# GpSimd takes eight weight splits and the pooling sums, the convolution sums in PSUM, and a layer norm's sums move into the stage before

## The chip, the cores and the metric

The kernel runs on one NeuronCore of a Trainium2 chip, with fp32 inputs and outputs. The metric is the device time of one execution in microseconds (us); lower is better. The kernel before was timed in 3 runs; one further execution was recorded by the hardware profiler.

## What is computed

The program is a stack of two layers (a retention layer, then a latent-attention layer, each followed by a per-layer embedding gate `x = x + sigmoid(x @ w_gate) * proj`) and then a second block with adaptive modulation. The change lies at the end of the second gate and in the first half of the second block, on 256 tokens of 1024 features. With `mod` worked out from a conditioning vector, that half computes:

```python
h  = layer_norm(x) * (1 + scale_1) + shift_1
z  = h @ w_in2                       # 4 x 512 channels: a, b for the GLU, c for the pool, then 2048 gates
u  = a * sigmoid(b)                  # GLU, 512 channels
v  = causal_depthwise_conv(u, 31 taps) + b_dw
v  = silu(layer_norm(v, g_a, b_a)) @ w_pw
q_g = sums of 2, 4, 8, 16 past tokens / width - c    # one group of 128 channels per width
q  = (q @ w_pool) * pool_scale
m  = sigmoid(gates_1) * v + sigmoid(gates_2) * q
x  = layer_norm(alpha * x + g_1 * (m @ w_out2), g, b)   # alpha = 2 ** 0.25
```

## The kernel before

Activations lie with features on the 128 partitions and the 256 tokens along the free axis, in blocks of 4 x 256 columns (tiles `half`). Weights come from DRAM in 258 tiles of 128 x 1024 fp32 (tiles `raw`), in one order, by DMAs that SyncE issues (L165). A tile holds eight 128 x 128 weights.

A product is made in one of two ways. An **fp32 tile** goes to TensorE as it is, one fp32 matmul for each weight (`mm32`, L243). A **split tile** is first taken apart: ScalarE casts it to fp32r (`hi`, tile `wh`, L178), VectorE subtracts that from the original (`lo`, tile `wl`, L179), and each product then is three fp32r matmuls, `hi` by `hi`, `hi` by `lo` and `lo` by `hi` (`mm`, L237 to L239). The raw tiles have 6 buffers, `wh` and `wl` 5 each; every second fp32 tile (by its place in the DRAM order) lies in a buffer of `wh`.

The stages around the change, in the order of TensorE's work:

- `ple_gate1`: eight output blocks; for each, `fin` (L697 to L699) takes a sigmoid on ScalarE, then a product and a sum on VectorE that give the new `x`. Blocks come in pairs (0,1), (2,3), (4,5) and then 6 and 7 alone.
- the part of `w_in2` that needs no norm yet (`ahead_mm`, L1011): 4 blocks of `w_in2` times `x * scale` (written by ScalarE at L1036), 32 fp32 matmuls of 258 columns. The layer norm's sums over `x` and its squares (`ln_sums`, L973; `sum_mm`, L363; matmuls with a matrix of ones) come in between, due 4.16 us of the program's own clock after the stage's beginning. Then `ln_stats`, `modulate` (L981) and `glu_ahead` (L1109), which takes the mean and the factor into the blocks that were multiplied ahead.
- `k_outer` (L1025): four split tiles, the other two channel groups of the GLU.
- the pool's two pairs of blocks, called P0 and P1 here (two tiles each), and the eight gates G0 to G7 (two tiles each, `in_tile` L1129), with `pool_out` (four small products with `w_pool`) after G3. Of these only G2, G5 and G6 are split (the bits of the number 100). Each gate ends with a sigmoid of 512 columns out of its PSUM bank (L1210).
- beside them the convolution (`conv_steps`, L1075): 2 channel pairs x 31 taps, one step each 0.9 us of the program's clock. A step is two multiplications on ScalarE (L1087) and one addition of 512 columns on VectorE (L1088), or, for some steps, two fused multiply-adds on VectorE (L1091). Its sums lie in SBUF.
- the pool (`pool`, L1145): 1, 2, 3 and 4 shifted additions on VectorE (L1150), then a tail of three operations (L1152, L1154, L1155) and a split (L187, L188) for `pool_out`.
- the norm of the convolution's result (`ln_a`; its first half's sums at L1170 in G2, the second's at L1178 in G7), then `w_pw` and `w_out2`. For the residual, `alpha * x` is written by ScalarE ahead of the convolution (`ax`, L1120).

GpSimd has hardly any work here: it clears 16 columns ahead of each pool tile (L1065).

The order within an engine comes from a queue of due times (`after(us, fn)`, read by `tick`, which TensorE's work moves forward) and from a scheduler that then places the recorded instructions. PSUM has 8 banks (`bank`, `bank2`).

## Time and profile before

| | |
|---|---|
| runs | 840.65, 841.06, 841.72 us; median 841.06 us |
| profiled execution | 839.76 us, of which the trace spans 838.0 us |
| granted TensorE clock | 0.996 of full speed |
| TensorE busy | 822.8 us, 98% of the span |
| VectorE, ScalarE, GpSimd busy | 84%, 66%, 1% |
| matmuls | L237, L238, L239: 1504 each of 256 columns; L243: 384 |

The profiled execution is read for durations and for who waits for whom; a row gives the start, the time, the engine, the line, the operation and the tiles. Rows of the same kind that follow each other are put together (x4). In the windows the busy share of each engine stands beside the stretch's length.

### The profile page before, as it was taken

To read this page: it belongs to the slowest core of one execution; us is meant where nothing else is said; L and a number is where in the kernel's file an instruction comes from. 1 tells how busy PE (TensorE), PEld (TensorE's weight loads), DVE (VectorE), ACT (ScalarE), POOL (GpSimd) and SP (SyncE) were. 2 spreads that over 40 slices of the span, in tenths; PEclk is the share of its full clock that TensorE was granted. 3 is DMA by queue.
4 is the path that set the end of the run, shared out by engine and by line. 5 is a ranking of instruction groups with operands and counts; after the bars stand their busy time and mean duration, and the time that the engine had idled before them with its cause. 6 is when DMAs were issued, how large, how long until landed. Compare 5 with 4: busy or idle time off the path is not lost.

```text
span 838.0 us, 15757 instructions
## 1 busy us (share of the span) xinstructions
PE 822.8 (98%) x6114; PEld 786.4 (94%) x6114; DVE 701.5 (84%) x1283; ACT 550.6 (66%) x966; POOL 9.9 (1%) x30
## 2 busy tenths in 40 slices
...
GB/s 332 328 249 228 205 228 271 248 261 316 174 174 241 273 135 286 111 224 198 114 175 187 116 201 180 72 176 199 129 250 121 136 195 180 190 211 240 285 80 76
DMA packets 46635, 167.49 MB, mean 200 GB/s; under 512 B 5216, under 2 KB 5472, under 8 KB 46560
## 3 DMA queue, kind: packets, MB, share of 16 engines
...
HBM read 165.41 MB, written 1.05 MB: 199 GB/s over the span
## 4 chain that ended last, share of the span: by engine, by line
PE 85%; DVE 7%; DMA 5%; ACT 1%; issue 1%; SPq 0%; DVEq 0%; POOL 0%; POOLq 0%; ACTq 0%
PE ps L238 24%; PE ps L239 23%; PE ps L237 23%; PE ps L243 11%; DVE wl L179 2%; DMA adach<-in_wada 1%; PE ps L341 1%; DMA g<-mod 1%; PE ps L363 1%; DMA half<-in_rows 1%; DMA half<-in_xT 1%; PE ps L920 1%; ACT wh L178 1%; DMA raw<-in_wts 1%; DMA half<-g 1%
## 5 line engine op out<-in xcount | busy, mean ns | idle before, releaser
L237 PE MATMUL ps<-half,wh 128*128 128x256 f32 x1504 | 424.9, 283 | 0.1
L238 PE MATMUL ps<-half,wh 128*128 128x256 f32 x1504 | 423.3, 282 | 0.7 <-DVE half L188 0.6
L239 PE MATMUL ps<-half,wl 128*128 128x256 f32 x1504 | 421.8, 281 | 0.0
L178 ACT CAST wh<-raw 128x1024 fp32r<-128x1024 f32 x233 | 243.2, 1049 | 147.4 <-PE ps L238 99.0
L179 DVE TENSOR_TENSOR wl<-raw,wh 128x1024 fp32r<-128x1024 f32 x233 | 282.2, 1218 | 55.4 <-ACT wh L178 53.6
L238 PEld LDWEIGHTS ps<-half,wh 128*128 128x128 f32 x1504 | 283.2, 188 | 2.0 <-DVE half L188 1.0
L237 PEld LDWEIGHTS ps<-half,wh 128*128 128x128 f32 x1504 | 282.7, 188 | 1.2 <-ACT half L187 0.5
L239 PEld LDWEIGHTS ps<-half,wl 128*128 128x128 f32 x1504 | 283.6, 189 | 0.0
L243 PE MATMUL ps<-half,raw 128*128 128x256 f32 (+2 forms) x384 | 84.9, 380 | 0.0
L243 PEld LDWEIGHTS ps<-half,raw 128*128 128x128 f32 x384 | 72.5, 190 | 10.0
L237 PE MATMUL ps<-wh,half 128*128 128x512 f32 (+1 forms) x202 | 72.6, 360 | 1.2 <-ACT wh L178 1.2
L238 PE MATMUL ps<-wl,half 128*128 128x512 f32 (+1 forms) x202 | 70.9, 351 | 0.5 <-DVE wl L179 0.5
L239 PE MATMUL ps<-wh,half 128*128 128x512 f32 (+1 forms) x202 | 71.0, 351 | 0.0
L413 DVE CUSTOM_DVE_ANT_0 adach<-adach,siluc 128x1024 f32<-128x1024 f32 x48 | 58.4, 1219 | 14.0 <-DMA adach<-in_wada 13.8
L1087 ACT ACTIVATE t<-apad,vec 128x256 f32<-128x256 f32 x106 | 44.2, 498 | 0.5 <-DVE half L1088 0.5
L237 PEld LDWEIGHTS ps<-wh,half 128*128 128x128 f32 x202 | 37.9, 188 | 7.0 <-ACT wh L178 2.0
L238 PEld LDWEIGHTS ps<-wl,half 128*128 128x128 f32 x202 | 38.1, 189 | 6.0 <-DVE wl L179 1.0
L239 PEld LDWEIGHTS ps<-wh,half 128*128 128x128 f32 x202 | 38.0, 188 | 5.5
L1088 DVE TENSOR_TENSOR half<-half,t 128x512 f32<-128x512 f32 x53 | 36.4, 686 | 3.7 <-ACT t L1087 1.8
L187 ACT CAST half<-t 128x256 fp32r<-128x256 f32 (+1 forms) x47 | 20.3, 453 | 14.3 <-DVE t L1347 11.1
L188 DVE TENSOR_TENSOR half<-t,half 128x256 fp32r<-128x256 f32 (+1 forms) x47 | 21.6, 481 | 4.3 <-ACT half L187 3.4
L1342 ACT ACTIVATE t<-ps,vec 128x256 f32<-128x256 f32 x38 | 21.0, 558 | 4.2 <-DVE t L1344 2.9
...
## 6 DMA issues: line engine op xcount, KB each, us to landing
raw<-in_wts SPq DMA_DIRECT2D x257, 512.0 KB, 4.3
adach<-in_wada SPq DMA_DIRECT2D x48, 512.0 KB, 5.3
...
half<-in_rows POOLq DMA_DIRECT2D x2, 512.0 KB, 5.6
...
siluc<-in_cv SPq DMA_DIRECT2D x1, 512.0 KB, 8.4
```

Of the source, the lines that this page charges most:

```text
L178: A.copy(hi, raw)
L179: V.tensor_sub(lo, raw, hi.bitcast(F32))
L187: A.copy(hi, src)
L188: V.tensor_sub(lo, src, hi.bitcast(F32))
L237: T.matmul(ps, l[0], r[0], start=first, stop=False)
L238: T.matmul(ps, l[0], r[1], start=False, stop=False)
L239: T.matmul(ps, l[1], r[0], start=False, stop=last)
L243: T.matmul(ps, w, r, start=first, stop=last)
L413: V.tensor_tensor_reduce(ch, ch, sc, 1.0, 0.0, MUL, ADD, mod[:, n:n + 1])
L1087: A.activation(t[:, b, :], apad[:, i0 + b, k:k + S], AF.Copy, scale=w[b])
L1088: V.tensor_add(acc.pair(i0 // 2), acc.pair(i0 // 2), t)
L1342: A.activation(t[:, b, :], ps[:, b, :], AF.Identity, bias=col("b_dw_f_2", m), scale=w[2])
```

## The change

- **Splits on GpSimd.** `load` takes a pair of engines (`by`). With `(G, G)` GpSimd casts the tile and subtracts. That holds for eight tiles: P1's two and those of G1, G3 and G5. Before, P1, G1 and G3 were fp32 tiles (six) and G5 was split by ScalarE and VectorE. G2 and G6 stay as they were; P0, G0, G4 and G7 stay fp32.
- **Pooling sums on GpSimd.** The 10 shifted additions of 256 columns.
- **Convolution in PSUM.** Each channel pair's sums lie in a PSUM bank of their own (`accp`); only the last tap writes to SBUF.
- **The norm's sums fed early.** `fin` of `ple_gate1` hands each new piece of `x` to a running sum (`Sums.feed`: a square on ScalarE, additions on VectorE). `flush` is due 4.16 us after blocks 4 and 5: it runs an `Abs_reciprocal_sqrt` on one column (`warm`), folds the two sums of squares into one in place, and starts the matmuls with ones. Blocks 6 and 7 come in by `end`. Six matmuls take the place of eight.
- **Alpha out of the residual.** `ax` goes; `w_out2`'s result is scaled by `g_1 / alpha`, and the next norm's epsilon by `1 / alpha ** 2`.
- **Gates ahead.** `modulate` of blocks 0 to 5 comes first, then `glu_ahead` for both blocks, then the rest.

```diff
     def load(entries, width, parts=True, raw=None, by=None):
...
-        A.copy(hi, raw)
-        V.tensor_sub(lo, raw, hi.bitcast(F32))
+        first, second = by or (A, V)
+        if first is G:
+            G.tensor_copy(hi, raw)
+        else:
+            A.copy(hi, raw)
+        second.tensor_sub(lo, raw, hi.bitcast(F32))
...
+    sumt = Sums(True, 1)
+    st = {}
+
+    def seen(x, k):
+        if k < 6:
+            sumt.feed(x)
+            if k == 4:
+                after(4.16, sumt.flush)
+        elif k == 6:
+            after(2.2, lambda: sumt.end(x, False))
+        else:
+            after(2.3, lambda: stats_in(x))
...
-    after(4.16, stats_in)
     pab = ahead_mm("w_in2", [0, 4, 1, 5], xs, 2)
...
-    modulate(xt, 0, mu, nrl, range(2), hp, hraw)
+    modulate(xt, 0, mu, nrl, range(3), hp, hraw)
...
     acc = Blk(4)
+    accp = [bank2() for _ in range(2)]
...
+            own = accp[i0 // 2]
...
+                to = acc.pair(i0 // 2) if k == 30 else own
...
-                    V.tensor_add(acc.pair(i0 // 2), acc.pair(i0 // 2), t)
+                    V.tensor_add(to, own, t)
...
     glu_ahead(0)
-    modulate(xt, 0, mu, nrl, range(2, 4), hp, hraw)
     glu_ahead(1)
-    ax = Blk(DB)
-    for i in range(4):
-        A.activation(ax.pair(i), xt.pair(i), AF.Copy, scale=ALPHA)
+    modulate(xt, 0, mu, nrl, range(3, 4), hp, hraw)
...
-            in_tile(ps[:, b, :], 8 + 2 * i + b, False)
+            in_tile(ps[:, b, :], 8 + 2 * i + b, i > 0, (G, G))
...
-            V.tensor_add(n[:, 16:], s[:, 16:], s[:, 16 - (1 << i):16 + S - (1 << i)])
+            G.tensor_add(n[:, 16:], s[:, 16:], s[:, 16 - (1 << i):16 + S - (1 << i)])
...
-        in_tile(ps[:, b, :], 12 + 2 * j + b, bool(100 >> i & 1))
+        in_tile(ps[:, b, :], 12 + 2 * j + b, i not in (0, 4, 7), (G, G) if i % 2 else None)
...
+    V.tensor_scalar(ga, mod[:, 16:24], 1.0 / ALPHA, None, MUL)
...
-            V.scalar_tensor_tensor(z[k], ps[:, b, :], mod[:, 16 + k:17 + k], ax[k], MUL, ADD)
+            V.scalar_tensor_tensor(z[k], ps[:, b, :], ga[:, k:k + 1], xt[k], MUL, ADD)
...
-        st["z"] = ln_stats(sumz.ps[::-1], D)
+        st["z"] = ln_stats(sumz.ps[::-1], D, (eps_a, LN_EPS / ALPHA ** 2))
```

What this does to the order of the instructions is shown at three places. Line numbers in these rows are those of the kernel they come from; the numbers behind names tell buffers apart.

**TensorE and ScalarE where `ple_gate1` ends.** On TensorE before: in the middle of `ahead_mm` (`ps_6373` to `ps_6376`, L243) stand the eight matmuls with ones; `ps_6391` takes the sums of `x`, `ps_6392` those of its squares.

```order
L243 MATMUL ps_6373<-half_6359,raw_6387 128x258 [waits Activation_49]
L243 MATMUL ps_6374<-half_6359,raw_6387 128x258
L363 MATMUL ps_6391<-t_1134_6403,ones 128x256 [waits DVE_49,PE_49]
L363 MATMUL ps_6391<-t_1134_6403,ones 128x256
L363 MATMUL ps_6391<-half_6086,ones 128x256 x2
L363 MATMUL ps_6392<-t_1130_6393,ones 128x256 [waits PE_49]
L363 MATMUL ps_6392<-t_1130_6393,ones 128x256
L363 MATMUL ps_6392<-t_1133_6401,ones 128x256 [waits Activation_49]
L363 MATMUL ps_6392<-t_1133_6401,ones 128x256
L243 MATMUL ps_6375<-half_6359,raw_6387 128x258
```

In the changed kernel, right behind the last matmul of `ple_gate1` (L244 into `ps_6330`); `ps_6355` takes the squares' sums (`t_1101` is the folded tile), `ps_6356` those of `x`; L248 is `ahead_mm`.

```order
L244 MATMUL ps_6330<-half_6060,wl_6334 128x256
L339 MATMUL ps_6355<-t_1101_6215,ones 128x256 [waits DVE_49,PE_49]
L339 MATMUL ps_6356<-t_1104_6224,ones 128x256 [waits PE_49]
L339 MATMUL ps_6355<-t_1126_6366,ones 128x256 [waits Activation_49]
L339 MATMUL ps_6356<-half_6088,ones 128x256
L248 MATMUL ps_6398<-half_6384,raw_6402 128x258 [waits DMAHW7_49,PE_49]
L248 MATMUL ps_6399<-half_6384,raw_6402 128x258 [waits PE_49]
L248 MATMUL ps_6400<-half_6384,raw_6402 128x258 [waits PE_49]
L248 MATMUL ps_6401<-half_6384,raw_6402 128x258 [waits PE_49]
L248 MATMUL ps_6398<-half_6384,raw_6402 128x258
L248 MATMUL ps_6399<-half_6384,raw_6402 128x258
L339 MATMUL ps_6355<-t_1135_6410,ones 128x256 [waits Activation_49]
```

Four of the matmuls with ones now stand ahead of all of `ahead_mm` and the first of them waits for VectorE; the last two follow six matmuls later. On ScalarE before, around the sigmoid of block 7 (L697), with the multiplications by `scale` (L1036) and the squares (L296):

```order
L1036 ACTIVATE half_6359<-half_6085,s_6352 128x256
L697 ACTIVATE t_1119_6348<-ps_6317 128x256 [waits PE_49]
L1036 ACTIVATE half_6360<-half_6086,s_6352 128x256 [waits DVE_49]
L1036 ACTIVATE half_6360<-half_6086,s_6352 128x256
L1036 ACTIVATE half_6360<-half_6086,s_6352 128x256 [waits DVE_49] x2
L296 ACTIVATE t_1130_6393<-half_6085 128x512
L296 ACTIVATE t_1131_6395<-half_6085 128x512
L296 ACTIVATE t_1132_6398<-half_6086 128x512
```

and in the changed kernel (L1046 the multiplications, L315 `warm`, which reads the tile `t_1101` that the fold writes, L355 the squares of blocks 6 and 7, L695 the sigmoid):

```order
L1046 ACTIVATE half_6384<-half_6087,s_6377 128x256 x3
L315 ACT_TABLE_LOAD
L315 ACTIVATE sm_6357<-t_1101_6215,eps_r 128x1 [waits DVE_49]
L355 ACTIVATE t_1126_6366<-half_6088 128x256 [waits DVE_49,Activation_49]
L695 ACT_TABLE_LOAD
L695 ACTIVATE t_1127_6373<-ps_6330 128x256 [waits PE_49]
L1046 ACTIVATE half_6384<-half_6087,s_6377 128x256
L1046 ACTIVATE half_6385<-half_6088,s_6377 128x256 x3
L1046 ACTIVATE half_6385<-half_6088,s_6377 128x256 [waits DVE_49]
L355 ACTIVATE t_1135_6410<-half_6088 128x256 [waits Activation_49]
```

Two loads of an activation table stand around `warm`, one ahead of it and one ahead of block 7's sigmoid; before there was none between the sigmoids.

**GpSimd, and VectorE ahead of G2.** On GpSimd in the changed kernel, from G1's second tile (`wh_6936`, `wl_6937`) on; `lv` are the pool's tiles, `upad` its input:

```order
L181 CAST wh_6936<-raw_6934 128x1024 [waits DMAHW1_49,DMAHW7_49,DMAHW0_49,PE_49]
L184 TENSOR_TENSOR wl_6937<-raw_6934,wh_6936 128x1024 [waits Pool_49]
L1155 TENSOR_TENSOR lv_6868<-upad 128x256 [waits Activation_49]
L1155 TENSOR_TENSOR lv_6946<-upad 128x256 [waits Activation_49]
L1069 MEMSET lv_6949 128x16 [waits DVE_49,Pool_49]
L1155 TENSOR_TENSOR lv_6949<-lv_6946 128x256 [waits Pool_49]
L1069 MEMSET lv_7064 128x16 [waits Pool_49]
L1069 MEMSET lv_7067 128x16 [waits DVE_49]
L1155 TENSOR_TENSOR lv_7064<-upad 128x256 [waits Activation_49]
L1155 TENSOR_TENSOR lv_7067<-lv_7064 128x256 [waits Pool_49]
L1069 MEMSET lv_7070 128x16 [waits Pool_49]
L1155 TENSOR_TENSOR lv_7070<-lv_7067 128x256
```

Before, GpSimd had in this stretch only the MEMSETs of 16 columns:

```order
L1065 MEMSET lv_6875 128x16 [waits DVE_49]
L1065 MEMSET lv_6955 128x16 [waits DVE_49]
L1065 MEMSET lv_6958 128x16 [waits DVE_49,Pool_49]
L1065 MEMSET lv_6961 128x16 [waits DVE_49]
L1065 MEMSET lv_7035 128x16 [waits DVE_49]
```

Behind these rows the changed kernel has the rest of the pool's additions, then the casts and subtractions for G3 and G5. On VectorE before, ahead of the subtraction for G2's first tile (`wl_6909`):

```order
L1155 TENSOR_TENSOR half_6791<-sm_6965,upad 128x16 [waits DVE_49]
L1150 TENSOR_TENSOR lv_7038<-lv_7035 128x256 [waits DVE_49,Pool_49]
L1088 TENSOR_TENSOR half_6482<-half_6482,t_1231_6867 128x512 [waits DVE_49]
L1091 SCALAR_TENSOR_TENSOR half_6482<-apad,vec,half_6482 128x256 [waits Activation_49]
L1088 TENSOR_TENSOR half_6482<-half_6482,t_1236_6888 128x512 [waits DVE_49]
L179 TENSOR_TENSOR wl_6909<-raw_6906,wh_6908 128x1024 [waits DMAHW6_49,Activation_49]
L1088 TENSOR_TENSOR half_6482<-half_6482,t_1237_6895 128x512 [waits DVE_49]
```

and in the changed kernel, ahead of the same subtraction (now `wl_6991`; `lv_7196` is the last of the pool's tiles that GpSimd writes, L1097 a convolution step):

```order
L1157 SCALAR_TENSOR_TENSOR half_6833<-lv_7196,upad 128x240 [waits Pool_49]
L1097 TENSOR_TENSOR ps_6498<-ps_6498,t_1232_6884 128x512 [waits DVE_49,Activation_49]
L193 TENSOR_TENSOR half_6837<-half_6833,half_6836 128x256 [waits Activation_49]
L1097 TENSOR_TENSOR ps_6498<-ps_6498,t_1237_6901 128x512 [waits DVE_49]
L1159 TENSOR_TENSOR sm_7200<-lv_7196,cst 128x16
L1237 TENSOR_SCALAR sm_7674<-gs 128x8
L1097 TENSOR_TENSOR ps_6498<-ps_6498,t_1238_6914 128x512 [waits DVE_49]
L1160 TENSOR_TENSOR half_6833<-sm_7200,upad 128x16 [waits DVE_49]
L1238 SCALAR_TENSOR_TENSOR sm_7674<-s_6377,vec 128x8
L1097 TENSOR_TENSOR ps_6498<-ps_6498,t_1239_6927 128x512 [waits DVE_49]
L184 TENSOR_TENSOR wl_6991<-raw_6988,wh_6990 128x1024 [waits DMAHW1_49,PE_49,Activation_49]
```

Before, the pool's additions (L1150) were VectorE's own and its fourth tail came behind this subtraction; now all four tails stand ahead of it, the fourth waits for GpSimd, and the convolution's steps write `ps_6498`.

**TensorE where G4 begins.** Before, the last product of `pool_out` (`ps_7107`) and G4 (`ps_7120`):

```order
L239 MATMUL ps_7107<-half_6794,wl_7070 128x256
L237 MATMUL ps_7107<-half_6794,wh_7069 128x256
L238 MATMUL ps_7107<-half_6795,wh_7069 128x256
L239 MATMUL ps_7107<-half_6794,wl_7070 128x256
L243 MATMUL ps_7120<-half_6454,raw_7121 128x256 [waits DMAHW6_49,Activation_49]
```

and in the changed kernel (`ps_7229`, `ps_7242`):

```order
L244 MATMUL ps_7229<-half_6836,wl_7174 128x256
L242 MATMUL ps_7229<-half_6836,wh_7173 128x256
L243 MATMUL ps_7229<-half_6837,wh_7173 128x256
L244 MATMUL ps_7229<-half_6836,wl_7174 128x256
L248 MATMUL ps_7242<-half_6460,raw_7243 128x256 [waits DMAHW7_49,Activation_49]
```

In both, G4's first matmul waits for ScalarE, whose sigmoid frees the PSUM bank. By the built programs' bank numbers `ps_7120` had G2's bank (`ps_6905`), while `ps_7242` has G3's (`ps_7090`), the one that was filled just before `pool_out`.

## Rows read from the trace of the kernel before

**Rows 1.** Parts 1, 4 and 6 of the page: busy time, share of the span and instructions of TensorE; the chain of work that ended last, by engine; and from part 6 SyncE's DMAs of weight tiles (count, KB each, median us from issue to landing).

```profile
PE 822.8 (98%) x6114; PEld 786.4 (94%) x6114; DVE 701.5 (84%) x1283; ACT 550.6 (66%) x966; POOL 9.9 (1%) x30
...
PE 85%; DVE 7%; DMA 5%; ACT 1%; issue 1%; SPq 0%; DVEq 0%; POOL 0%; POOLq 0%; ACTq 0%
...
raw<-in_wts SPq DMA_DIRECT2D x257, 512.0 KB, 4.3
```

**Rows 2.** The windows of the stretches: the norm's stage, `k_outer`, P0 and P1, G0 and G1 (length, busy time and instructions of each engine, granted clock, DMA share, GB/s).

```profile
496.62:514.13 17.51, 17.51 (x82) 15.11 (x82) 13.71 (x25) 12.88 (x30) 0.00 (x0) 1.00 0.45 151
514.13:525.43 11.30, 11.30 (x97) 11.30 (x97) 6.60 (x17) 11.27 (x28) 0.00 (x0) 1.00 0.54 187
525.43:539.25 13.82, 13.82 (x66) 12.17 (x65) 12.65 (x25) 13.67 (x36) 0.12 (x1) 1.00 0.12 39
539.25:552.68 13.43, 13.43 (x64) 11.80 (x63) 13.43 (x33) 13.01 (x31) 0.67 (x6) 1.00 0.33 118
```

**Rows 3.** The chain of waits, in order of time (start, us, what): the longest pieces between 496 and 554 us. Every fp32 matmul is recorded as two, so x128 are the 64 matmuls of eight tiles, and x16 are eight sums.

```profile
496.62 6.10 PE ps L243 x28
502.71 3.58 PE ps L363 x16
506.29 7.83 PE ps L243 x36
525.43 27.63 PE ps L243 x128
```

**Rows 4.** ScalarE's timeline at the end of `ple_gate1` and in the norm's stage (start, us; in brackets idle time before it and what ended it).

```profile
493.72 1.05 ACT L178 CAST wh<-raw 128x1024 fp32r<-128x1024 f32 x1 [1.32 <-issue]
...
494.68 0.37 ACT L697 ACTIVATE t<-ps 128x256 f32<-128x256 f32 x1
494.95 0.28 ACT L1008 COPY half<-s 128x4 f32<-128x4 f32 x2
...
495.32 1.70 ACT L1036 ACTIVATE half<-half,s 128x256 f32<-128x256 f32 x4
...
505.28 1.28 ACT L393 ACT_TABLE_LOAD   x1
...
509.93 0.60 ACT L991 ACTIVATE half<-t,mod,ms 128x256 fp32r<-128x256 f32 x1 [2.14 <-DVE t L987]
```

**Rows 5.** VectorE's timeline in the same place: the last sums that give `x`.

```profile
493.81 0.69 DVE L699 TENSOR_TENSOR half<-t,half 128x512 f32<-128x512 f32 x1
...
497.32 0.42 DVE L698 TENSOR_TENSOR t<-t,half 128x256 f32<-128x256 f32 x1 [0.50 <-ACT t L697]
497.79 0.42 DVE L699 TENSOR_TENSOR half<-t,half 128x256 f32<-128x256 f32 x1
```

**Rows 6.** ScalarE's groups by line and shape (busy us, mean ns of one, idle before): casts of weights and `warm` over the whole span, `ax` and the norm's squares from 484 to 600 us.

```profile
L178 ACT CAST wh<-raw 128x1024 fp32r<-128x1024 f32 x233 | 243.2, 1049 | 147.4 <-PE ps L238 99.0 <-issue 24.2 <-PE ps L239 15.0
...
L317 ACT ACTIVATE sm<-t,eps_r 128x1 f32<-128x1 f32 x4 | 1.2, 306 | 0.0
...
L1120 ACT ACTIVATE half<-half 128x512 f32<-128x512 f32 x4 | 2.3, 625 | 0.0
...
L296 ACT ACTIVATE t<-half 128x512 f32<-128x512 f32 x4 | 2.2, 616 | 0.0
```

**Rows 7.** VectorE's groups over the whole span: the convolution's additions, the fused multiply-adds, the weights' subtractions, a pool addition, and an addition that reads PSUM.

```profile
L1088 DVE TENSOR_TENSOR half<-half,t 128x512 f32<-128x512 f32 x53 | 36.4, 686 | 3.7 <-ACT t L1087 1.8
...
L179 DVE TENSOR_TENSOR wl<-raw,wh 128x1024 fp32r<-128x1024 f32 x233 | 282.2, 1218 | 55.4 <-ACT wh L178 53.6
...
L1091 DVE SCALAR_TENSOR_TENSOR half<-apad,vec,half 128x256 f32<-128x256 f32 x14 | 6.2, 478 | 0.2
...
L1150 DVE TENSOR_TENSOR lv<-lv 128x256 f32<-128x256 f32 x6 | 2.5, 414 | 0.0
...
L548 DVE SCALAR_TENSOR_TENSOR t<-ps,t 128x512 f32<-128x512 f32 x8 | 5.5, 684 | 0.3 <-PE ps L239 0.3
```

**Rows 8.** GpSimd's operations: the only two that read and compute (minimum, median and maximum ns of one), and two forms of MEMSET.

```profile
L1432 POOL TENSOR_TENSOR t<-t,half x2: 1253/1495/1737, 828.6 to 830.3; 128x512 f32<-128x512 f32 x2
...
L767 POOL MEMSET kr<- 64x256 f32 x4 | 1.2, 306 | 149.0 <-DVE t L560 148.8
...
L1065 POOL MEMSET lv<- 128x16 f32 x10 | 1.1, 112 | 134.1 <-DVE sm L1154 122.1 <-DVE lv L1150 12.0
```

**Rows 9.** The timelines of GpSimd and VectorE around those two operations.

```profile
828.58 2.96 POOL L1432 TENSOR_TENSOR t<-t,half 128x512 f32<-128x512 f32 x2 [11.89 <-DVE t L1431]
...
827.81 1.38 DVE L1431 TENSOR_TENSOR t<-t,half 128x512 f32<-128x512 f32 x2
...
831.31 0.77 DVE L1434 SCALAR_TENSOR_TENSOR t<-t,sm,half 128x512 f32<-128x512 f32 x1
...
832.08 0.74 DVE L1434 SCALAR_TENSOR_TENSOR t<-t,sm,half 128x512 f32<-128x512 f32 x1
```

**Rows 10.** Around the gates: VectorE's subtraction for G2's first tile, on ScalarE the square of the convolution's first half and the sigmoid of G3, and on TensorE the beginning of `w_pw`.

```profile
550.76 1.21 DVE L179 TENSOR_TENSOR wl<-raw,wh 128x1024 fp32r<-128x1024 f32 x1
...
552.66 0.63 ACT L1165 ACTIVATE t<-half 128x512 f32<-128x512 f32 x1 [0.32 <-DVE half L1088]
...
568.44 0.58 ACT L1210 ACTIVATE half<-ps 128x512 f32<-128x512 f32 x1
...
597.13 0.73 PE L237 MATMUL ps<-half,wh 128*128 128x256 f32 x4
```

53 lines of the change are left out of this document (22 added, 31 removed).

## The prediction

> **What bounds the kernel now.** I read the page's busy shares and its chain first: TensorE is busy 98% of the span, and 85% of the chain of waits is TensorE's [rows 1]. So the time is TensorE's work plus its waits, and an edit counts only by what it does to these. Then the windows of the changed stretch: TensorE works without a gap from 496.62 to 552.68, at a granted clock of 1.00, the 2.4 GHz level [rows 2]. In the same windows ScalarE has 13.67 of 13.82 us and VectorE 13.43 of 13.43: they are nearly full, so a delay on one of them soon reaches TensorE. Last the chain by pieces, for the price of a matmul in each form [rows 3].
>
> **Six tiles split (P1, G1, G3).** Eight fp32 tiles take 27.63 us in a row [rows 3], 3.454 each. `k_outer` does four split tiles in 11.30 us [rows 2], 2.825 each. The difference is 0.629, six times that is **-3.77 us**, all of it on TensorE's path if no wait takes its place. G5 is split already; moving its two splits takes 2 casts of 1.05 [rows 6] from ScalarE and 2 subtractions of 1.22 [rows 7] from VectorE, nothing from TensorE.
>
> **The norm's stage.** The eight sums take 3.58 us [rows 3], 0.448 each; six take 2.68, so -0.90. The 32 products of `ahead_mm` (6.10 + 7.83 us [rows 3], 0.435 each) stay. But four sums now stand ahead of all of them, and the first waits for the fold, which writes in place what `warm` reads, and `warm` needs its table. Laying out ScalarE's rows in the new order: the cast from 493.72 ends at 494.8 [rows 4]; the square of blocks 4 and 5 takes 0.62 [rows 6], its input is there at 494.50 [rows 5], so 495.4; the sigmoid of block 6 takes 0.37 and the four copies 0.37 [rows 4], which brings it to 496.1; three multiplications at 0.41 (four in 1.70 [rows 4]) to 497.2 or 497.3; the table 1.28 [rows 4] to 498.5; `warm` 0.31 [rows 6] to 498.8; the fold 0.42 like the addition of that size [rows 5] to 499.2. TensorE is there at 496.62 and **waits 2.6 us**. Then four sums (501.0), six products (503.6), two sums (504.5) and 26 products: `k_outer` starts at 515.8, where it was 514.13. The term is **+1.7 us**. It can't be much more, since after that the stage runs on TensorE alone (the first `modulate`, at 509.93 before [rows 4], gets its sums some 1.8 us sooner). Its lower end is a fold that waits for VectorE alone, with block 6's sum shortly before block 7's product at 497.32 [rows 5]: a wait of about 1.1, a term of +0.2; with no wait at all, -0.9. I take 1.7, since the order shows the wait.
>
> [...]
>
> **Convolution in PSUM, alpha, gates ahead.** A VectorE operation of 512 columns takes 684 ns with an input in PSUM and 686 without [rows 7]; one that also writes PSUM isn't in the trace. I take no difference. Were each of the 53 additions 10% slower, the convolution would end 3.6 us later, by which the second half of `ln_a` would hold `w_pw` up; that end is in the range. `ax` (four copies of 0.62 [rows 6]) goes from ScalarE, where it stood ahead of the first tap, so the convolution can begin two us sooner against the start of `k_outer`. That cancels the later start; I cost both at nothing. The new scale factor is one small operation.
>
> **GpSimd's own time.** Two inputs of 512 columns took it 1253 ns without company [rows 8], 2.45 ns a column; a MEMSET 306 ns for 256 columns and 112 for 16 [rows 8], 0.81 ns a column. So an estimate of 2.4 us for a subtraction of 1024 columns and 0.65 to 0.7 for a pool addition. A cast has one input: between 0.93 (MEMSET's slope) and 2.4 (two inputs). I take 1.1, as one input is nearer to the MEMSET, with 2.4 as the other end.
>
> Does this hide? P1's tiles: the buffers come free as `k_outer` goes through its tiles (from 518.6 every 2.8 us), a split takes 3.5, and TensorE is at P1 at 515.8 + 11.3 + 6.9 = 534.0. G1's: the second needs the `wh` buffer of P0's first tile (free at 530.6) and is done at 534.1, needed at 549.4. Then the pool: three additions on P0's output, seven on P1's (there at 539.7, plus copies), with their MEMSETs, end near 546, and the fourth tail on VectorE follows. G2's subtraction stands behind that tail: 550.1 to 551.3, against 550.76 before [rows 10]. TensorE needs it at 515.8 + 11.3 + 13.8 + 11.3 = 552.2. **It hides, with 0.9 us to spare.** If the cover goes, TensorE waits at G2 for the excess. SyncE's order is the same, but its issues for G2's and G3's tiles now wait for GpSimd's subtractions of P1 and G1 (526 and 534) where they waited for TensorE; a tile lands 4.3 us after its issue [rows 1], before the casts for G2 and G3 come up (some 546).
>
> **G4's PSUM bank.** G4 now takes the bank of G3, whose sigmoid must first be done. Before, from the square of the convolution's first half (552.66) to that sigmoid (568.44) ScalarE took 15.78 us [rows 10]; now two more multiplications and one cast and one half split fewer lie between, some 15.4. The first half ends at about 553.1 (its last taps stand behind the fourth tail), so the sigmoid ends near 569.1 (0.58 [rows 10]). TensorE reaches G4 at 552.2 + four tiles 11.3 + sums 1.7 + `pool_out` 2.8 = 568.0: **+1.1 us**, between 0 and 1.7.
>
> **The sum.** 839.76 - 3.77 + 1.7 + 1.1 = 838.8 for an execution like the profiled one. The runs' median lies 1.30 above it (841.06), so **840.1 us**: 0.1% faster than before. A difference under 0.2% (839.4 to 842.7) can't be told from none.
>
> **Rivals.**
>
> *Short waits, a plain gain.* If the fold waits for VectorE only (+0.2) and ScalarE reaches G3's sigmoid in time (0), the sum is 839.76 - 3.57 + 1.30 = 837.5. With no wait in the norm's stage it would be 836.4. For it: all windows show an ordered flow, and the additions and subtractions that leave VectorE (10 x 0.41 and 2 x 1.22 [rows 7]) are 6.5 us of slack. Against it: the tables stand in the order.
>
> *GpSimd and VectorE block each other (slower).* The first two-input operation of GpSimd began at 828.58, while VectorE's second of two with both inputs in SBUF ran to 829.19; the two took 2.96 together, one 1253 and one 1737 [rows 8, 9]. The excess of 0.48 is close to the 0.6 that VectorE still had to go. Against it: VectorE's 831.31 began 0.23 before GpSimd's end and took 0.77 against the next one's 0.74 [rows 9]. The convolution's steps have one input in PSUM and would be spared; the pool's tails, the splits for `pool_out` and G2's subtractions, some 13 operations with two SBUF inputs between 534 and 553, are the ones that meet GpSimd's additions and G3's casts. Half an addition (0.35) at ten of them and half a cast or a subtraction (0.6 to 1.2) at the others give about 5 us on VectorE's queue, of which 0.9 is spare: TensorE waits 4 us at G2, the sum is 844.2. It decides from a delay of 0.9 us on.
>
> "SBUF — State Buffer" of the Trainium skill, section "Who interferes with whom", states this rule: a VectorE instruction with two SBUF inputs and a GpSimd instruction that reads SBUF exclude each other for a whole instruction, whichever came first, and one with at most one SBUF input is free. The trace agrees on GpSimd's side (1737 against 1253 ns) and doesn't on VectorE's (0.77 against 0.74).
>
> *GpSimd is slow.* With 2.4 for a cast and 2.7 for a subtraction the four splits of P1 and G1 run back to back from 518.6 at 5.1 each to 538.9, the pool's additions start 4.2 later, G2's subtraction ends 3.7 after TensorE wants it, and the sum is 843.8.
>
> *It doesn't do what it says.* That the fed sums bring nothing, since TensorE then waits for them, is part of the forecast already.
>
> **How the numbers follow.** The forecast (840.1; its own range 838.2 to 842, which takes in 0.2 to 2.2 for the norm's stage and 0 to 1.7 for the bank) has 0.42, a third of it under 839.4, as its lower bounds reach further than its upper ones. Short waits 0.25. Blocking 0.20, a quarter of it under 842.7. Slow GpSimd 0.10. Slow writes to PSUM (843.7 by the 3.6 us above) 0.03. So faster is 0.14 + 0.25 = 0.39, slower 0.15 + 0.10 + 0.03 = 0.28, and no difference that can be told 0.33. The range reaches from 836.4, the sum without a wait in the norm's stage or at G4, to 845.0, a little over the blocking.
>
> **What would show it.** The norm's stage: a TensorE wait for the fold of about 2.6 us right after `ple_gate1`, and three table loads on ScalarE between 494 and 508. The tiles: P1, G1 and G3 at 5.65 us each. The hiding: no TensorE wait at P1, G1, G2 or G3, and GpSimd's cast near 1.1 us. The bank: a wait of about 1 us of G4 for ScalarE. Blocking would show as VectorE's pool tails and subtractions longer than 0.4 and 1.22, or late without a visible releaser, and a wait at G2 for `wl`. The prediction falls if the stretch from 496.6 to `w_pw` (597.1 before [rows 10]) changes by over 3 us either way.

## The result, and the profile after

| | before | changed |
|---|---|---|
| runs | 841.39 us median (840.65 to 842.26, 4 runs) | 851.65 us median (850.58 to 853.36, 4 runs) |
| profiled span | 838.0 us | 851.6 us |
| `ple_gate1`'s last matmul to `w_pw` | 496.62 to 597.13: 100.51 us | 497.95 to 610.12: 112.17 us |

The ratio is 1.0133, with a 95% interval from 1.0116 to 1.0151: 1.3% slower. Where `ple_gate1` ends varies by some us (495.48 to 501.91 in profiled executions of kernels that are alike up to there), so the stretch from there to `w_pw` is the better measure, and below each run is read by it (called the stretch). It grew by 11.66 us, in place of shrinking by about 1. One execution of each kernel gives it, so it isn't exact either: p1_fp32 below has a stretch 4.7 us shorter than the changed kernel's, and a median only 1.0 us lower.

The page's part 1 of the changed kernel, which answers to [rows 1]:

```profile
PE 825.5 (97%) x6158; PEld 790.3 (93%) x6158; DVE 709.1 (83%) x1275; ACT 549.8 (65%) x964; POOL 44.2 (5%) x56
```

TensorE has fewer fp32 matmuls and yet 2.7 us more busy time, and GpSimd's 44.2 us are no large share. What TensorE waited for, between 480 and 620 us (the engine's instructions, released by; us in total, times, longest):

```profile
PE ps L244 <- DVE wl L184: 6.0, 1, 6.0
PE ps L339 <- DVE t L348: 2.7, 1, 2.7
PE ps L242 <- ACT half L192: 1.4, 1, 1.4
PE ps L243 <- DVE half L1008: 1.2, 1, 1.2
```

Four waits, where there was none before: at G2 for VectorE's `lo` (6.0), at the sums for the fold (2.7), at `w_pw` (1.4) and in `k_outer` (1.2). And the windows (columns as in [rows 2]; the granted clock stands third from the end), cut at these waits:

```profile
497.95:500.69 2.74, 0.00 (x1) 0.03 (x1) 1.78 (x5) 2.69 (x6) 0.00 (x0) 1.00 0.50 190
500.69:504.25 3.56, 3.56 (x9) 2.85 (x10) 0.85 (x2) 3.55 (x8) 0.00 (x0) 0.53 0.00 1
504.25:519.00 14.75, 14.75 (x69) 12.87 (x69) 10.48 (x18) 9.32 (x17) 0.00 (x0) 1.00 0.40 143
...
557.10:563.36 6.26, 0.23 (x3) 0.03 (x2) 6.26 (x9) 2.33 (x5) 4.36 (x2) 0.92 0.00 0
563.36:566.00 2.64, 2.64 (x12) 2.64 (x13) 2.64 (x5) 1.08 (x3) 0.00 (x0) 0.50 0.55 200
566.00:572.10 6.10, 6.10 (x36) 5.92 (x34) 5.75 (x11) 6.10 (x15) 0.00 (x0) 0.74 0.88 340
```

After the waits of 2.7 and 6.0 us TensorE works at 0.53 and 0.50 of full speed for some us, the 1.2 GHz level, and 0.74 is a window with both levels. What that costs is busy time times the missing share: 3.56 x 0.47 + 2.64 x 0.50 + 6.10 x 0.26 = 4.6 us. With the waits (2.74 + 1.2 + 6.03 + 1.39 = 11.4) that is 16.0; the splits (-3.77) and the two sums saved (-0.90) leave 11.3 of the 11.66 us.

Why VectorE was late at G2 is read from its timeline beside GpSimd's, in `k_outer`. VectorE:

```profile
521.43 0.75 DVE L1061 SCALAR_TENSOR_TENSOR t<-t,t 128x256 f32<-128x256 f32 x2
522.10 0.86 DVE L1060 SCALAR_TENSOR_TENSOR t<-t,sm,ps 128x256 f32<-128x256 f32 x2
522.88 3.01 DVE L1061 SCALAR_TENSOR_TENSOR t<-t,t 128x256 f32<-128x256 f32 x2
525.81 1.26 DVE L1008 TENSOR_TENSOR half<-half,half 128x256 fp32r<-128x256 f32 x1
526.99 3.01 DVE L1122 SCALAR_TENSOR_TENSOR apad<-t,sm,t 128x256 f32<-128x256 f32 x2
529.92 0.41 DVE L1008 TENSOR_TENSOR half<-half,half 128x256 fp32r<-128x256 f32 x1
531.63 3.92 DVE L1097 TENSOR_TENSOR ps<-ps,t 128x512 f32<-128x512 f32 x5 [1.29 <-ACT t L1096]
```

and GpSimd with P1's two tiles, then G1's:

```profile
521.92 1.16 POOL L181 CAST wh<-raw 128x1024 fp32r<-128x1024 f32 x1 [99.43 <-PE ps L243]
523.16 2.44 POOL L184 TENSOR_TENSOR wl<-raw,wh 128x1024 fp32r<-128x1024 f32 x1
525.56 1.23 POOL L181 CAST wh<-raw 128x1024 fp32r<-128x1024 f32 x1
526.87 2.45 POOL L184 TENSOR_TENSOR wl<-raw,wh 128x1024 fp32r<-128x1024 f32 x1
531.90 1.04 POOL L181 CAST wh<-raw 128x1024 fp32r<-128x1024 f32 x1 [2.58 <-PE ps L243]
533.02 2.37 POOL L184 TENSOR_TENSOR wl<-raw,wh 128x1024 fp32r<-128x1024 f32 x1
```

L1061 and L1122 belong to `glu_ahead`. Two L1061 take 0.75 us alone, and 3.01 when GpSimd's subtraction (523.16 to 525.60) lies beside them: the pair ends at 525.89, just behind it. The next, a subtraction of 256 columns (0.41 alone), takes 1.26 and ends just behind the second cast; then two L1122 take 3.01 and end behind the second subtraction. The operation between them with an input in PSUM (L1060, two in 0.86) and later the convolution's (L1097, five in 3.92, beside G1's splits) take their usual time. So five operations with both inputs in SBUF cost VectorE some 5 us (3.01 - 0.75, 1.26 - 0.41 and 3.01 - 0.97). The convolution's first addition comes at 531.63; before it was

```profile
524.48 5.49 DVE L1088 TENSOR_TENSOR half<-half,t 128x512 f32<-128x512 f32 x7 [1.83 <-ACT t L1087]
```

That is 7.15 us later, but 4.87 of it is the start of `k_outer` (514.13 before, 519.00 now). Against that start the convolution is 2.3 us late; the rest of the 5 us is made up, presumably by `ax`, which is gone from ahead of the first tap. Ahead of G2 the same repeats with operations of 16 columns:

```profile
554.53 1.21 DVE L1157 SCALAR_TENSOR_TENSOR half<-lv,upad 128x240 f32<-128x240 f32 x1 [1.20 <-POOL lv L1155]
...
557.44 1.74 DVE L1159 TENSOR_TENSOR sm<-lv,cst 128x16 f32<-128x16 f32 x1
...
559.77 1.72 DVE L1160 TENSOR_TENSOR half<-sm,upad 128x16 f32<-128x16 f32 x1
...
562.09 1.21 DVE L184 TENSOR_TENSOR wl<-raw,wh 128x1024 fp32r<-128x1024 f32 x1
```

The first of these waits 1.20 us for GpSimd's last pool addition, and each of 16 columns takes 1.7 us (0.16 alone) while GpSimd casts and subtracts for G3. G2's subtraction starts at 562.09, where it was 550.76 [rows 10]: 11.3 us later, to which `ple_gate1`'s end gives 1.3, the norm's stage 3.5, the convolution's start 2.3 and this tail some 5 (1.20, 0.8, 1.6 and 1.6), a little more in sum. Last `w_pw`. ScalarE in the changed kernel, and then in the kernel before:

```profile
604.70 0.51 ACT L391 ACTIVATE t<-t,eps_l 128x256 f32<-128x256 f32 x1
607.39 1.28 ACT L1191 ACT_TABLE_LOAD   x1 [2.18 <-DVE t L1188]
608.68 1.09 ACT L1191 ACTIVATE t<-t,vec,lng 128x256 f32<-128x256 f32 x2
```

```profile
593.04 0.51 ACT L393 ACTIVATE t<-t,eps_l 128x256 f32<-128x256 f32 x1
593.57 1.28 ACT L1186 ACT_TABLE_LOAD   x1
595.69 1.09 ACT L1186 ACTIVATE t<-t,vec,lng 128x256 f32<-128x256 f32 x2 [0.84 <-DVE t L1183]
```

Before, the load of Silu's table ran first and the activation waited for VectorE; now the load itself stands behind the wait, and the 1.28 us come on top.

### The profile page after: what moved, and what is told of

The parts are those of the page before. It is cut to its first block, busy times and chain, and to the rows that moved or that the text cites. A ratio compares the mean times of both kernels' runs of the same rounds, so it can differ in the third digit from the quotient of the medians.

```text
span 851.6 us, 15869 instructions
## 1 busy us (share of the span) xinstructions
PE 825.5 (97%) x6158; PEld 790.3 (93%) x6158; DVE 709.1 (83%) x1275; ACT 549.8 (65%) x964; POOL 44.2 (5%) x56
## 3 DMA queue, kind: packets, MB, share of 16 engines
HBM read 165.41 MB, written 1.05 MB: 195 GB/s over the span
## 4 chain that ended last, share of the span: by engine, by line
PE 81%; DVE 10%; ACT 3%; DMA 3%; issue 2%; POOL 0%; SPq 0%; DVEq 0%; POOLq 0%; ACTq 0%
PE ps L243 25%; PE ps L244 24%; PE ps L242 24%; PE ps L248 5%; DVE ps L1097 2%; PE ps L339 2%; DVE wl L184 1%; DMA g<-mod 1%; DMA half<-in_xT 1%; DMA half<-in_rows 1%; PE ps L920 1%; DMA half<-g 1%; PE ps L361 1%; DVE t L1319 1%; DVE t L1061 0%
## 5 line engine op out<-in xcount | busy, mean ns | idle before, releaser
L244 PE MATMUL ps<-half,wl 128*128 128x256 f32 x1552 | 436.2, 281 | 6.0 <-DVE wl L184 6.0
L242 PE MATMUL ps<-half,wh 128*128 128x256 f32 x1552 | 439.6, 284 | 1.4 <-ACT half L192 1.4
L243 PE MATMUL ps<-half,wh 128*128 128x256 f32 x1552 | 438.4, 283 | 1.8 <-DVE half L1008 1.2
L244 PEld LDWEIGHTS ps<-half,wl 128*128 128x128 f32 x1552 | 293.7, 189 | 6.2 <-DVE wl L184 6.2
L243 PEld LDWEIGHTS ps<-half,wh 128*128 128x128 f32 x1552 | 293.5, 189 | 3.3 <-DVE half L1008 1.7
L242 PEld LDWEIGHTS ps<-half,wh 128*128 128x128 f32 x1552 | 292.8, 189 | 2.5 <-ACT half L192 1.8
L243 PE MATMUL ps<-wl,half 128*128 128x512 f32 (+1 forms) x202 | 71.7, 355 | 0.5 <-DVE wl L184 0.5
L244 PE MATMUL ps<-wh,half 128*128 128x512 f32 (+1 forms) x202 | 71.7, 355 | 0.0
L411 DVE CUSTOM_DVE_ANT_0 adach<-adach,siluc 128x1024 f32<-128x1024 f32 x48 | 58.4, 1218 | 12.6 <-DMA adach<-in_wada 12.5
L248 PE MATMUL ps<-half,raw 128*128 128x256 f32 (+2 forms) x288 | 64.4, 381 | 0.0
L248 PEld LDWEIGHTS ps<-half,raw 128*128 128x128 f32 x288 | 54.6, 191 | 7.7
L243 PEld LDWEIGHTS ps<-wl,half 128*128 128x128 f32 x202 | 38.4, 190 | 6.2 <-DVE wl L184 1.0
L244 PEld LDWEIGHTS ps<-wh,half 128*128 128x128 f32 x202 | 38.4, 190 | 5.7
L1097 DVE TENSOR_TENSOR ps<-ps,t 128x512 f32<-128x512 f32 x51 | 35.5, 696 | 4.3 <-ACT t L1096 1.3
## 6 DMA issues: line engine op xcount, KB each, us to landing
cst<-in_cst SPq DMA_DIRECT2D x1, 928.0 KB, 10.3
```

What stands on the lines that cost most here:

```text
L242: T.matmul(ps, l[0], r[0], start=first, stop=False)
L243: T.matmul(ps, l[0], r[1], start=False, stop=False)
L244: T.matmul(ps, l[1], r[0], start=False, stop=last)
L248: T.matmul(ps, w, r, start=first, stop=last)
L411: V.tensor_tensor_reduce(ch, ch, sc, 1.0, 0.0, MUL, ADD, mod[:, n:n + 1])
L1097: V.tensor_add(to, own, t)
```

## Experiments

The theory: GpSimd's reads of SBUF shut out VectorE's operations with two SBUF inputs, in `glu_ahead` above all. The first rival: the norm's stage and the pool's way through GpSimd made the time. All numbers together (stretch, waits and lost time come from one profiled execution; "half clock" is busy time times the missing share of the clock over the stretch, read in windows of 2 us; waits stand in order of time, those of 0.2 us are left out, 2.7 is the wait at the sums, 1.4, 0.6 and 0.8 are at `w_pw`, others of 1.2 to 2.1 without a place in `k_outer`):

| run | median us | ratio to before, 95% | stretch | TensorE's waits | half clock |
|---|---|---|---|---|---|
| changed | 851.65 | 1.0116 to 1.0151 | 112.17 | 2.7, 1.2, 6.0 (G2), 1.4 | 4.4 |
| sums_old | 850.96 | 1.0097 to 1.0141 | 109.71 | 2.1, 7.2 (G2), 1.4 | 2.0 |
| p1_fp32 | 850.66 | 1.0090 to 1.0155 | 107.47 | 2.7, 1.9 (G2), 3.4 (G4) | 1.6 |
| pool_dve | 850.46 | 1.0095 to 1.0132 | 110.12 | 2.7, 1.2, 3.6 (G2), 1.4 | 4.6 |
| conv_sbuf | 862.98 | 1.0238 to 1.0299 | 124.00 | 2.7, 1.3, 3.8 and 12.9 (G2), 0.6 | 6.4 |
| sums_late | 848.80 | 1.0083 to 1.0130 | 108.92 | 2.1, 5.7 (G2), 1.4 | 3.4 |
| splits_av | 853.64 | 1.0132 to 1.0179 | 110.59 | 2.7, 1.2 (a cast), 1.9 (`lo`, two), 0.4, 5.5 (`w_pw`) | 1.6, and 2.6 after `w_pw` begins |
| late_no_gpsimd | 841.43 | 0.9991 to 1.0020 | 101.28 | 1.4 (`w_pw`) | 0.0 |
| g1_g5_gpsimd | 842.70 | 1.0019 to 1.0046 | 102.17 | 1.9 (G4), 1.4 | 0.0 |
| late_fix | 841.66 | 0.9997 to 1.0024 | 99.97 | none | 0.0 |
| g1_fix | 838.78 | 0.9972 to 0.9995 | 98.71 | none | 0.0 |
| p1_only | 842.48 | 0.9997 to 1.0043 | 102.65 | 2.1 (`k_outer`) | 1.5 |
| before_reads | 861.87 | 1.0229 to 1.0271 | 122.88 | 11.1 and 6.9 (G2), 0.8 | 3.5 |
| before_reads1 | 853.65 | 1.0102 to 1.0177 | 115.57 | 8.2 and 3.4 (G2) | 3.4 |
| before_writes | 840.64 | 0.9982 to 1.0013 | 100.52 | none | 0.0 |
| reads_alone | 850.79 | 1.0098 to 1.0146 | 109.50 | 5.2 (G2), 1.4 | 2.5 |
| writes_alone | 840.73 | 0.9991 to 1.0022 | 101.85 | 1.4 (`w_pw`) | 0.0 |

### Parts undone: the norm's sums, P1, the pool, the convolution

**sums_old**, the sums of the kernel before:

```diff
-    xt = post(xt, ys, sums, 1, prep, seen)
+    xt = post(xt, ys, sums, 1, prep)
...
+    after(4.16, stats_in)
```

> The changed kernel with the norm's sums back where they were (eight sums in the middle of the products ahead, no feeding in the gate's stage, no warm-up of the table between the sigmoids). Theory: in the changed kernel the norm's stage took 21.0 us (497.95 to 519.0) against 17.5 before, because TensorE waited 2.74 for the fold behind the table and then ran the four sums at half clock (3.56 us for 1.79). Undone, the stage is 17.5 again and the median goes from 851.65 to about 848.1. Rival: the stage's loss is covered by the later wait at G2 (convolution and pool set the end, not TensorE), so the wait at G2 grows by what is gained: 851 to 852.

**p1_fp32**, P1's tiles as fp32 tiles:

```diff
-            in_tile(ps[:, b, :], 8 + 2 * i + b, i > 0, (G, G))
+            in_tile(ps[:, b, :], 8 + 2 * i + b, False)
```

> The changed kernel with the pool's second pair of blocks (P1) left as two fp32 tiles, so that GpSimd has no work until the gates' tiles; all else as changed. Theory (GpSimd and VectorE exclude each other): VectorE's operations for the GLU ahead (L1061 up to 1.5 us, L1122 1.54) then take 0.42 and 0.48 again, the convolution begins 4 to 5 us sooner after the products ahead, the 1.2 us wait of k_outer for L1008 goes, and the wait at G2 shrinks from 6.0 to 1 to 2 us without a stretch at half clock; two fp32 tiles cost 1.26. Sum about 843.5 to 846. Rival (GpSimd is only late in its queue, no exclusion): the pool's additions wait for the same output of P1 as now, so G2 waits as long as now: 852 to 853.

**pool_dve**, the pool's additions back on VectorE:

```diff
-            G.tensor_add(n[:, 16:], s[:, 16:], s[:, 16 - (1 << i):16 + S - (1 << i)])
+            V.tensor_add(n[:, 16:], s[:, 16:], s[:, 16 - (1 << i):16 + S - (1 << i)])
```

> The changed kernel with the pool's ten additions back on VectorE; the eight splits stay on GpSimd. Theory (exclusion): the late convolution and the tails blocked by G3's casts and subtractions (L1159 and L1160 at 1.7 us each) stay or move, VectorE gets 4.1 us more work ahead of G2; 850 to 854. Rival (the pool's chain through GpSimd is what G2 waits for): the fourth tail no longer waits for GpSimd, G2's wait shrinks by 2 us or more: 848 or less.

**conv_sbuf**, the convolution's sums in SBUF while GpSimd has its new work:

```diff
-            own = accp[i0 // 2]
+            own = acc.pair(i0 // 2)
```

> The changed kernel with the convolution's sums in SBUF again, all else as changed. Theory (exclusion, only for VectorE operations with two inputs in SBUF): each convolution step that meets a GpSimd operation waits for it or makes it wait; GpSimd is busy some 35 us between 522 and 581, so steps of 0.7 us grow and GpSimd's splits too; the kernel gets 8 to 20 us slower, 860 to 872. Rival (no exclusion, or PSUM is what costs): 849 to 852.

None of the first three brings the time back; undone alone, each leaves a loss of 1.1 to 1.2%, as the others' delays then end last. The theory had expected shorter times for two of them (848.1 for sums_old, 843.5 to 846 for p1_fp32). sums_old is without the 2.7 us wait, but its waits in `k_outer` and at G2 are 0.9 and 1.1 us longer, so its time is near what the rival said; the stretch gives 2.46 back, of which 2.3 is clock. pool_dve's wait at G2 is 2.4 us shorter, as its rival said, while its time stays where the theory had it: the pool's way through GpSimd is a part of that wait. Without P1's splits the stretch is 4.7 us shorter although 1.26 us of TensorE's gain go with them. But 1.7 of the 4.7 lie ahead of P1: behind the same wait of 2.74 us at the sums, TensorE worked at 1.00 in this execution (504.65 to 508.20), where the changed kernel has 0.53. So P1 isn't clearly a larger part than the pool. In VectorE's groups for `glu_ahead` in p1_fp32 (behind the bar busy us, mean ns)

```profile
L1061 DVE SCALAR_TENSOR_TENSOR t<-t,t 128x256 f32<-128x256 f32 x4 | 1.5, 420 | 0.0
L1122 DVE SCALAR_TENSOR_TENSOR apad<-t,sm,t 128x256 f32<-128x256 f32 x2 | 0.9, 484 | 0.1
```

the means are 420 and 484 ns again, where pool_dve keeps 981 and 1540, and the convolution's first addition (528.99) comes 7.9 us after `k_outer`'s first matmul (521.05), where the changed kernel has 12.9 (531.63 and 518.78). G4 then waits 3.4 us for its PSUM bank: ScalarE, whose sigmoid frees it, had been idle for 7.2 us until VectorE was through with the convolution's first half. conv_sbuf shows which operations are open to it: with both inputs in SBUF the additions take

```profile
L1096 DVE TENSOR_TENSOR half<-half,t 128x512 f32<-128x512 f32 x53 | 51.4, 970 | 4.4 <-ACT t L1095 1.3
```

970 ns where the changed kernel's 51 with a PSUM input take 696 on the same work beside the same GpSimd, and the stretch is 11.8 us longer. So the sums in PSUM did their part: without them the stretch is 23.5 us over before, twice the changed kernel's 11.66.

### The norm's stage later, and GpSimd without work

**sums_late** gives the fold and its six sums later due times, which puts them behind eleven of `ahead_mm`'s products:

```diff
-                after(4.16, sumt.flush)
+                after(8, sumt.flush)
...
-            after(2.2, lambda: sumt.end(x, False))
+            after(6, lambda: sumt.end(x, False))
...
-            after(2.3, lambda: stats_in(x))
+            after(3.5, lambda: stats_in(x))
```

> The changed kernel with the fed sums placed later only: the fold, the table's warm-up and the six matmuls with ones are due after nine of the products ahead, when the last sigmoid is done. Theory: the wait of 2.74 us for the fold and the half clock behind it (some 1.8 us) go, the stage of the norm takes 16.6 to 17.5 us where it took 21.0; since the modulation and the convolution start sooner by less than that, a part of it comes back as wait at G2 (7 us or more). The stretch from the end of ple_gate1 to w_pw shrinks from 112.2 to 108 to 110 us. Rival (the early place of the sums is no loss by itself, G2 sets the time): stretch 112, G2 waits 10 us.

**splits_av** keeps the changed kernel and its pool on GpSimd, but ScalarE and VectorE make all splits (`(G, G)` left out).

> The changed kernel with all eight splits on ScalarE and VectorE (casts and subtractions), so GpSimd has only the pool's additions; sums as in the changed kernel. Theory: the GLU ahead is not blocked (L1122 at 0.48 us), the convolution begins as early as in p1_fp32; the six new splits put 6.3 us on ScalarE and 7.3 on VectorE, which were nearly full, the pool's additions take 4.1 from VectorE and block some tails. Stretch 106 to 110 us, with waits of TensorE for casts or subtractions of the gates. Rival (the blocking is all of the loss): the stretch takes 98 to 101 us plus the 3.6 of the norm's stage.

**late_no_gpsimd** is sums_late with nothing on GpSimd but the MEMSETs of 16 columns: P1, G1, G3 as fp32 tiles, the pool on VectorE. The convolution in PSUM, alpha and the gates ahead stay.

> All GpSimd work undone (P1, G1 and G3 fp32 tiles again, G5 split by ScalarE and VectorE, pool's additions on VectorE); fed sums placed later as in sums_late; convolution in PSUM, alpha out of the residual and gates ahead kept. Theory: without GpSimd's reads nothing is blocked, TensorE has no wait over 1 us in the stretch, which takes 99.6 to 101 us (two sums fewer, 0.9); the median is 0 to 1.5 us under that of before. Rival (writes to PSUM or the order of modulation cost the convolution its pace): waits at G2 or G4 of 2 us and more, stretch 103 or more.

**g1_g5_gpsimd** is that with G1's and G5's splits on GpSimd.

> late_no_gpsimd with the splits of G1 and G5 on GpSimd alone (G1's two tiles split instead of fp32), where VectorE has few operations with two inputs in SBUF: G1's splits fall into the stretch in which VectorE only adds the convolution's steps into PSUM. P1 and G3 stay fp32. Theory: no blocking of over 1 us in sum, two split tiles save 1.26, the stretch takes 98.3 to 99.7 us, 0.1 to 0.3% faster than before. Rival (GpSimd's splits slow VectorE whatever it does): VectorE's additions get longer than 0.75 us while GpSimd works, a wait of 2 us and more at G2.

sums_late takes the 2.7 us wait and the half clock behind it away (from 499.00 to 504.30, where the sums begin, the clock is at 1.00); 3.25 us of the stretch come back, more than the wait, though G2 still waits 5.7. late_no_gpsimd takes another 7.6 us away, and with them the waits at G2 and in `k_outer` and all of the half clock: it stands within 0.2% of before. So GpSimd's work as a whole makes the stretch 7.6 us longer, with the 3.77 that it saves on TensorE already in that number. splits_av shows that there is no room for these splits elsewhere either: TensorE then waits for the casts and for the half of the convolution that comes late (5.5 at `w_pw`). g1_g5_gpsimd missed its 98.3 to 99.7, and by the theory's own mechanism. G1's splits, beside the convolution in PSUM, cost VectorE nothing, but G5's come beside the pool's fourth tail. VectorE and ScalarE there:

```profile
556.51 1.99 DVE L1155 TENSOR_TENSOR lv<-lv 128x256 f32<-128x256 f32 x1
560.94 1.84 DVE L1160 TENSOR_TENSOR half<-sm,upad 128x16 f32<-128x16 f32 x1
562.81 0.41 ACT L192 CAST half<-half 128x256 fp32r<-128x256 f32 x1 [2.76 <-DVE half L1160]
```

The addition (0.42 alone) and the operation of 16 columns (0.16 alone) end with GpSimd's two subtractions or just behind, at 558.5 and 562.8. ScalarE is idle for 2.76 us behind the second and comes to G3's sigmoid at 570.00, where late_no_gpsimd has it at 568.05: that is G4's wait of 1.9 us for its bank.

### Mending what is left, and P1 by itself

**late_fix** is late_no_gpsimd with a Silu of one column on the norm's factor, which loads the table while ScalarE is idle:

```diff
+        if then:
+            then(r0)
...
-        mu, nrl = ln_stats(la["ps"], 512)
+        mu, nrl = ln_stats(la["ps"], 512, then=lambda r: A.activation(small(1), r[:, 0:1], AF.Silu))
```

> The changed kernel without GpSimd's work and with the norm's sums behind the products (841.43 in its run), plus a Silu of one column on the factor's tile in ln_a, so that the table loads while ScalarE would be idle. If the table load that had come behind the semaphore makes the 1.39 us wait at w_pw, that wait goes and the stretch from ple_gate1 to w_pw is 99.7 to 100.2 where it was 101.28, the time 839.8 to 840.5, 0.1 to 0.2% under before. Rival: something else is late there (VectorE's factor), and the wait stays between 0.8 and 1.4.

**g1_fix** is late_fix with G1's two tiles split by GpSimd, **p1_only** late_fix with P1's two.

> The same, and G1's two tiles split by GpSimd alone (before: fp32 tiles), while VectorE has the pool's tails and the convolution in PSUM; G5 stays with ScalarE and VectorE, G3 an fp32 tile. Two tiles save 1.26 us on TensorE. If G4's bank, whose sigmoid comes some 1.9 us late with GpSimd's two gates, eats that again, the time is that of the run beside it or up to 0.5 us over it; if not, the stretch is 98.5 to 99.0 and the time 838.5 to 839.5, 0.2 to 0.3% under before. Exclusion alone would cost VectorE 1 to 3 us in two-input operations between 531 and 539, which is no wait unless G2's subtraction is reached late.

> The mended kernel without GpSimd's work (841.66 in its run, stretch 100.25), and P1's two tiles split by GpSimd, as in the change. TensorE saves 1.26 us. By the theory that these splits shut out the operations with two SBUF inputs that work out the GLU of the two groups multiplied ahead, these operations grow (L1061's kind from 420 to over 900 ns, L1122's kind from 484 to over 1400), the convolution begins 3 to 5 us later, and TensorE waits 1 to 5 us at G2 or G4: the stretch is 100.5 to 104. By the rival that it takes the pooling sums and G3's casts as well to make a wait, the stretch is 98.8 to 99.3 without a wait.

ScalarE in late_fix ahead of `w_pw`:

```profile
596.26 1.28 ACT L1186 ACT_TABLE_LOAD   x1
597.56 0.20 ACT L1186 ACTIVATE sm<-t 128x1 f32<-128x1 f32 x1
598.41 1.09 ACT L1193 ACTIVATE t<-t,vec,lng 128x256 f32<-128x256 f32 x2 [0.65 <-DVE t L1190]
```

The load is ahead of the wait, the 1.39 us wait of TensorE is gone and the stretch is 1.31 shorter. The median isn't: 841.66, where 839.8 to 840.5 was expected. The runs' beginnings vary more than that (839.34 to 844.16 in 12 runs; `ple_gate1` ends at 499.88 in the profiled one and at 497.20 in the run that it is held against). g1_fix shortens the stretch by another 1.26, just the two tiles' gain, has no wait (G5's splits are ScalarE's and VectorE's again), and at 838.78 us is the fastest version: 0.16% under before, with 0.05 to 0.28% as its interval, so it beats both kernels, though by less than the 0.2% that the prediction called no difference. P1's two tiles in the same kernel gain the same on TensorE and lose it: VectorE in p1_only

```profile
515.21 3.44 DVE L1063 SCALAR_TENSOR_TENSOR t<-t,t 128x256 f32<-128x256 f32 x2
518.57 0.86 DVE L1062 SCALAR_TENSOR_TENSOR t<-t,sm,ps 128x256 f32<-128x256 f32 x2
519.36 2.98 DVE L1063 SCALAR_TENSOR_TENSOR t<-t,t 128x256 f32<-128x256 f32 x2
522.26 0.41 DVE L1010 TENSOR_TENSOR half<-half,half 128x256 fp32r<-128x256 f32 x1
```

beside GpSimd

```profile
515.91 2.46 POOL L184 TENSOR_TENSOR wl<-raw,wh 128x1024 fp32r<-128x1024 f32 x1
518.32 1.23 POOL L181 CAST wh<-raw 128x1024 fp32r<-128x1024 f32 x1
519.63 2.42 POOL L184 TENSOR_TENSOR wl<-raw,wh 128x1024 fp32r<-128x1024 f32 x1
```

Each pair (L1063 here) ends just behind GpSimd's subtraction, four operations take 6.4 us in place of 1.5, and L1010, which `k_outer`'s next products need, is late: TensorE waits 2.12 us and then has the clock at 0.56 for 3.9 us. The wait came at another place than expected (`k_outer`, not G2 or G4), since GpSimd began its casts 19.7 us after `ple_gate1`'s end here (at 514.78) and 24.0 after it in the changed kernel. The stretch: -1.26 + 2.1 + 1.5 = +2.3, measured +2.68 (102.65 against 99.97; the expectation has 100.25 for late_fix).

### GpSimd's reads and writes in the kernel before

To measure the dispute by itself, the kernel before gets work on GpSimd that nobody needs, beside the convolution's steps (whose sums lie in SBUF there):

```diff
     def conv():
         next(conv_it, None)
...
+        for _ in range(2):
+            nc.gpsimd.tensor_copy(sin4, apad[:, 0, 30:])
```

**before_reads** has copies, **before_writes** MEMSETs of the same size in their place.

> The kernel before, to which GpSimd gets 124 copies of 128x256 from the convolution's input into a tile that isn't used any more, two beside each convolution step (one more ahead of them); nothing waits for them but the tile's next writer, and TensorE, ScalarE and VectorE keep their orders. By the theory that GpSimd's reads of SBUF and VectorE's operations with two SBUF inputs shut each other out, the convolution's additions (two SBUF inputs here) grow from 686 ns to 850 to 1200, those with two inputs in the pool grow as well, the convolution comes late by 5 us or more and the kernel is slower by 3 to 12 us, with a TensorE wait at G2, G6 or w_pw. By the rival that GpSimd only was late for those who waited for it, the additions stay near 690 ns and the time is within 0.2%.

> The same with MEMSETs in place of the copies, so that GpSimd is as busy with instructions that read nothing. By the theory of exclusion by inputs the additions stay at 680 to 700 ns and the time is within 0.2% of before. By the rival that any work of GpSimd slows VectorE (or that the pool's own MEMSETs of 16 columns, queued behind the added ones, hold the pool up), this run and the one with copies are slowed alike.

before_writes came out as expected: its MEMSETs keep GpSimd busy for 38.6 us, and additions (689 ns) and time are those of before. before_reads was inconclusive on its price: additions grew to a mean of 765 ns only, and most of its 21 us came from another cause. The copies took 0.62 us each, GpSimd fell behind, and VectorE waited 12.5 us for a pool MEMSET of 16 columns that was queued behind them. **before_reads1**, with one copy a step, showed the same with 10.3 us (853.65 us, where 841 to 847 was expected). So in **reads_alone** and **writes_alone** VectorE clears the 16 columns itself, and nothing waits for GpSimd:

```diff
-        nc.gpsimd.memset(t[:, :16], 0.0)
+        nc.vector.memset(t[:, :16], 0.0)
```

> The kernel before with one copy of 128x256 on GpSimd beside each convolution step, 63 in all, into a tile that isn't used any more; the pool's MEMSETs of 16 columns are VectorE's, so nothing waits for GpSimd. By the theory of exclusion VectorE's operations with two SBUF inputs take 0.1 to 0.2 us more each while copies run (in the run before, additions 0.88 in place of 0.68, those of 16 columns 0.36 in place of 0.17), those with one PSUM input stay as they are (L1107's kind near 0.41); by G2's subtraction VectorE has lost 3.5 to 5 us, of which about 2 are spare, so TensorE waits 1.5 to 3 us at G2, runs at half clock for a while, and the time is 842.5 to 846. By the rival (queueing alone made those runs slow) no wait and within 0.2% of before.

> The same with MEMSETs of 128x256 in place of the copies (but for the first). Both theories expect no wait and a time within 0.2% of before; a time as late as that of the run with copies would speak against exclusion by inputs and for a cost of GpSimd's work of any kind, or of the eight MEMSETs that VectorE now does.

Groups by line (mean ns second behind the bar) of reads_alone, then of writes_alone: GpSimd's added work, the convolution's additions, the pool's operations of 16 columns, and an addition with an input in PSUM.

```profile
L1108 POOL COPY sin<-apad 128x256 f32<-128x256 f32 x62 | 39.5, 637 | 3.8
L1088 DVE TENSOR_TENSOR half<-half,t 128x512 f32<-128x512 f32 x53 | 38.9, 733 | 4.1 <-ACT t L1087 2.3
L1160 DVE TENSOR_TENSOR sm<-lv,cst 128x16 f32<-128x16 f32 x4 | 1.2, 310 | 0.0
L1113 DVE TENSOR_TENSOR apad<-ps,t 128x256 f32<-128x256 f32 x2 | 0.8, 411 | 0.0
```

```profile
L1108 POOL MEMSET sin<- 128x256 f32 x62 | 19.3, 312 | 3.6
L1088 DVE TENSOR_TENSOR half<-half,t 128x512 f32<-128x512 f32 x53 | 36.5, 688 | 4.1 <-ACT t L1087 1.8 <-DVE half L1088 0.5
L1160 DVE TENSOR_TENSOR sm<-lv,cst 128x16 f32<-128x16 f32 x4 | 0.7, 169 | 0.0
L1113 DVE TENSOR_TENSOR apad<-ps,t 128x256 f32<-128x256 f32 x2 | 0.8, 418 | 0.0
```

With writes beside them all four keep their time and the kernel too (1.0007 of before). With reads the operations with two SBUF inputs grow, those with a PSUM input don't, G2 waits 5.2 us and the kernel is 1.2% slower; the copies themselves take 637 ns in place of 396 (the one copy ahead of the steps). That is more than expected (842.5 to 846): the wait at G2 is 5.2 where 1.5 to 3 was expected, as GpSimd, slowed itself, went on past G2's subtraction, the half clock takes 2.5 and a table load behind its wait at `w_pw` 1.4. The last has nothing to do with the copies; writes_alone has it as well.

## Why the prediction was wrong

**The step that failed is "Does this hide?", with its "It hides, with 0.9 us to spare".** It laid GpSimd's work beside VectorE's as if VectorE's operations kept their times. The stretch was to shrink by 1.0 us and grew by 11.66; of the 12.6 between, the wait at G2 is 6.0, the half clock 4.4, `w_pw` 1.4 and the wait in `k_outer`, for a subtraction of `modulate` that came late behind P1's splits, 1.2, less the bank's 1.1. The rival on blocking had the mechanism and the place where it would be seen, a wait at G2 for `wl`, but was wrong in two ways. Its list of operations that meet GpSimd began at 534 and left `glu_ahead` out: five operations of 256 columns with both inputs in SBUF at 522 to 530, beside P1's splits, cost some 5 us; p1_fp32 and p1_only show that these are the ones. And it charged half an operation's time for each, where the rows show VectorE's operation ending with GpSimd's (a pair of 0.75 us in 3.01, one of 0.16 in 1.74). By its own charges (ten at 0.35, three at 0.6 to 1.2) the sum is 5.3 to 7.1, not about 5. Its "against it", the operation at 831.31 that took 0.77 us beside GpSimd [rows 9], was thin evidence: the two overlapped by 0.23 us only.

The rule of the Trainium skill, page "SBUF — State Buffer", section "Who interferes with whom", which the prediction named, is that a VectorE instruction with two SBUF inputs and a GpSimd instruction that reads SBUF contend for a shared port pair, an exclusive lock, and that a GpSimd instruction that only writes, or a VectorE instruction with at most one SBUF input outside the 2-port modes, doesn't. The traces here agree on both sides (VectorE 420 to 980 and 484 to 1544 ns, one PSUM input 696 beside 686; writes free). The condition on one input, which the prediction left out, may matter: in p1_fp32 a TENSOR_SCALAR of 8 columns with one SBUF input (L1237) took 1.05 us beside a cast of GpSimd, in the changed kernel 0.16. No run shows which mode it ran in.

**The norm's stage.** The wait was predicted at 2.6 us and is 2.74; the table loads and `warm` stand as laid out. The term was +1.7 and the stage (497.95 to `k_outer` at 519.0) takes 21.05 in place of 17.51 us, +3.5: the half clock behind the wait (1.7) was not in the sum. sums_late, without the wait, has the clock at 1.00 there; but so has p1_fp32 with the same wait, so the wait alone doesn't decide it, and what does is open.

**The clock.** No term of the sum held it, and no stretch of the trace before that was read has a wait on TensorE, so the rows gave no hint. Of the 11.66 us it is 4.4 to 4.6.

**`w_pw`** was not in the sum: the table load behind the semaphore, 1.28 us, which the trace of the changed kernel shows and the prediction didn't foresee.

**The tiles and GpSimd's durations were right.** A cast takes 1.04 us (1.1 predicted), a subtraction 2.37 (2.4), a pool addition 0.61 (0.65 to 0.7). g1_fix has the 1.26 us of its two tiles in full. **The convolution in PSUM** costs nothing (696 beside 686 ns), as taken, and it spared VectorE more than the prediction credited it with.

**The bank** was predicted at +1.1, and G2's wait hides it in the changed kernel. Where it shows, at 1.9 (g1_g5_gpsimd) and 3.4 us (p1_fp32), it is outside the predicted 0 to 1.7, but ScalarE had been idle for VectorE there, by 2.8 and 7.2 us: the same failed step, and not the count of ScalarE's work. Without GpSimd's work, and in g1_fix, G4 has no wait.

**The other rivals.** "GpSimd is slow" was wrong in its durations. "Short waits, a plain gain" fell with the fold's wait, slow writes to PSUM with the 696 ns. By its own test, a stretch that changes by over 3 us, the prediction fell: it changed by 11.66.

Not settled: how the 112.17 us divide between P1, the pool's additions and G3's casts. P1's splits and the additions give 4.7 (1.7 of it clock ahead of P1) and 2.1 when undone alone, but the waits hide behind each other, so these aren't shares of a sum, and G3's splits weren't undone alone.
